# Three small edits in a one-core hybrid encoder step: an earlier weight cast, ten moved sums, other PSUM banks for one product

## The chip, the cores and the metric

The kernel runs on one core of one Trainium2 chip. The metric is device time in microseconds: the median of several runs without a profiler. The core has five engines that run side by side, each through its own queue in order: TensorE (PE in the profile; its weight loads are PEld), VectorE (DVE), ScalarE (ACT), GpSimd (POOL) and SyncE (SP), which here only issues DMA transfers. Matmuls write into PSUM, which has eight banks of 2 KB for each of 128 partitions; all else lives in SBUF or in DRAM.

## The reference

One layer of a streaming encoder, applied to 1024 prompt frames and 32 sample frames that share the weights. Width D = 1024, all in float32:

```python
h = rms_norm(x, g_mix)
q, k, v, ch, cb, cc, ga, gb = split(h @ w_in)           # 1024 x 6656
a = window_attention(q, k, v, sink) @ w_attn_out         # 16 heads, 4 kv heads, ALiBi, sink
conv = causal_conv3(cc * ch)
bo = (cb * conv) @ w_conv_out
x = x + (sigmoid(ga) * a + sigmoid(gb) * bo) @ w_mix_out
hc = rms_norm(x, g_cross)
x = x + softmax(cq(hc) @ mem_k) @ mem_v @ w_co           # 4 heads over 256 memory tokens
hm = rms_norm(x, g_mlp)
x = x + square(relu(hm @ w_up)) @ w_down                 # hidden 4096
y = rms_norm(x, g_final)
```

Besides y it returns the last K and V rows, the last rows of the convolution's input and the memory's K and V.

## The kernel before, in words

**Tiling.** Activations stand with features on the 128 partitions and frames along the free axis, in three chunks of 384, 384 and 288 frames (`CH`). A feature block f is 128 features, so there are eight for each chunk. Every float32 product is made of three matmuls in a shorter float format: weights and activations are each split into a high part (`hi`, `wh`) and a low part (`lo`, `wl`), and hi x hi, hi x lo and lo x hi are added (`gemm`, `product`). A split is one ScalarE cast (L120) and one VectorE subtraction (L121). A weight block of 128 x 1024 is 512 KB; its raw form comes by SP into `wr` (two buffers), its parts go into `wh` and `wl` (three buffers each).

**Order.** Python code writes out the program in full; a planner (the tile framework's scheduler, with a simulated timeline) then sets each engine's order by the program's order and by what is ready in its simulation, and puts in the waits. What it sets is static: on the chip an engine waits at the head of its queue. `plan` is a list of items with the weights that they need; `next_w` issues weights two ahead. `events` is a hand-written table of 48 slots (16 products of three chunks each) beside which the attention units, copies and sums are put.

**Stages.** First the norm, Q, K, V and the memory's K and V; then the 16 products of `hosts`, with attention beside them; then the *input pairs*; then attention's output, convolution's output, mix and cross-attention chunk by chunk; then the up and down projections.

**Input pairs.** Fifteen pairs (`XP`) of output blocks of `w_in` are computed for the two chunks of 384 in a Strassen-Winograd manner: seven products in place of eight. `x_sums` makes from the activations the sums N3, N1, T2 and N4, `x_split` splits them. For a pair, `x_fetch` loads two raw weights (`wr`, and `wr2`), `pair_sums` makes two sums of weights (`s31` and `s24`, one buffer each; VectorE lines 866 and 869, POOL lines 867 and 868), and `x_issue(i, which)` splits weight 1 or 2 (the raw ones), 3 (`s31`) or 4 (`s24`). Weight 2 has buffers of its own; 1, 3 and 4 use the three `wh` and `wl`. `x_p1` and `x_p2` are the first and second half of a product with weight 1, `x_c2(i, half)` is the plain product of the third chunk, in the PSUM tag `pt`. `x_pair` does the rest: weight 4 with T2, weight 3 with N1 and N3, weight 4 with the second chunk's own activations, weight 2 with N4. `x_start` runs ahead: it does weight 1's work for pairs 0 and 1, which `x_pair` then leaves out by `early`. Names such as `x_issue(2, 1)` take the pair and the weight.

**Sums in DRAM.** The down projection needs sums of blocks of `w_down` (`wsum_d`). They are made in DRAM: per block four copies by SP and five DMA transfers by POOL that add what they read to what stands there (L736), 512 KB each, 40 in all. They are kept in program order by `pin`, and each waits for those that it builds on.

**PSUM.** In all stages up to the down projection the eight banks are `acc` (3 buffers of one bank), `pt` (2), `s` (one tile of two banks, scores of attention) and `o` (one bank, attention's values).

**Cross output product.** `do_co(c, half)` computes four feature blocks of the product with `w_co`, two at a time, for chunk c; VectorE adds each to the residual (L1276), and the squares are summed by ScalarE and POOL (`square_acc`, L250 and L252) for the next norm. For the second chunk (c = 1) the two halves run beside the last mix products of the third chunk.

Of the kernel before, what the change touches and what calls it, by code (L numbers as in the profile page):

```python
# [10 lines left out]
F32 = mybir.dt.float32  # L11
# [7 lines left out]
P = 128  # L19
# [19 lines left out]
def hybrid_step(ctx: ExitStack, tc: tile.TileContext, io):  # L39
# [5 lines left out]
    def nm(s):  # L45
        uid[0] += 1
        return f"{s}_{uid[0]}"

    def opened(name, **kw):
        cm = tc.tile_pool(name=name, **kw)  # L50
        return cm, cm.__enter__()

    def closed(cm):
        cm.__exit__(None, None, None)
# [7 lines left out]
    ps_cm, ps = opened("ps", bufs=1, space=PSUM)  # L62
# [28 lines left out]
    def acc_tile(shape):  # L91
        return ps.tile(shape, F32, tag="acc", bufs=n_acc, name=nm("acc"))
# [148 lines left out]
    def square_acc(x, f, c, on_pool=False):  # L241
        n = CH[c][1]
        if f == 0:
            accs[c] = [xacc[0][:, CH[c][0] : CH[c][0] + n]]
        acc = accs[c][0]
        sq = tmp(n) if f else acc
        if on_pool:
            pool_e.tensor_tensor(sq, x, x, op=ALU.mult)
        else:
            act.activation(sq, x, AF.Square)  # L250
        if f:
            pool_e.tensor_tensor(acc, acc, sq, op=ALU.add)  # L252
# [473 lines left out]
    def at(slot, fn):  # L726
        events.setdefault(slot, []).append(fn)
# [14 lines left out]
    adds = [x for s in range(len(sums) + 2) for ph in (2, 1, 0) if 0 <= s - ph < len(sums) for x in sums[s - ph][1][ph]]  # L742
# [12 lines left out]
            at(base + 11, lambda kv=kv: do_KS_rest(kv + 1))  # L755
    for i, x in enumerate(copies):
        at(2 + i, x)
    for i, x in enumerate(adds):
        at(8 + i, x)
    at(38, lambda: x_raw(0))  # L760
    at(40, lambda: x_sums(0))
    at(42, lambda: x_raw(1))
# [39 lines left out]
    def x_raw(k):  # L802
        if k == 0:
            two = [at_tile([P, NT], F32R, t, 2).bitcast(F32) for t in ("KSh", "KSl")]
        elif k == 1:
            two = [C["pool"].tile([P, 1060], F32, tag="u", name=nm("u")), at_tile([P, 4, 256], F32, "bias").rearrange("p h k -> p (h k)")]
        else:
            two = [S["xk"].tile([P, 768], F32, tag="xk", bufs=4, name=nm("xk")) for _ in range(2)]
        xr[k] = b12, b22, b11, b21 = [t[:, a : a + 384] for t in two for a in (0, 384)]
        for t, c, f in ((b12, 1, k), (b22, 1, k + 4), (b11, 0, k), (b21, 0, k + 4)):  # L810
            sp.dma_start(t, io[f"x{c}"][:, f])
# [37 lines left out]
    def pair_issue(key, which):  # L849
        if which == 4 and len(raws[key]) == 2:  # L850
            pair_sums(key)
        src = {1: 0, 2: 1, 3: 2, 4: 3}[which]
        if which == 2:
            hi, lo = (PW["pool"].tile([P, 1024], F32R, tag=t, name=nm(t)) for t in ("wh2", "wl2"))
        else:
            hi, lo = (wp.tile([P, 1024], F32R, tag=t, name=nm(t)) for t in ("wh", "wl"))
        split(hi, lo, raws[key][src])
        wset[key, which] = (hi, lo)
# [22 lines left out]
    def resume():  # L881
        if worder[wpos[0]] is STOP:
            wpos[0] += 1
        issue_w()
# [8 lines left out]
    def x_fetch(i):  # L893
        if i < len(XP):
            pair_fetch(("x", i), *(io["w_in"][in_col(t)] for t in XP[i]))

    def x_issue(i, which):
        if i < len(XP):
            pair_issue(("x", i), which)
        elif which != 2:  # L900
            resume()
# [14 lines left out]
    def x_p1(i):  # L916
        A = acc_tile([P, 384])
        product(A, x_w(i, 1), 0, [x11(k) for k in range(4)], True)
        s1 = xs1[i] = PW["pool"].tile([P, 384], F32, tag="s1", bufs=2, name=nm("s1"))
        act.copy(s1, A)  # L920
        return A

    def x_p2(i, A):
        product(A, x_w(i, 1), 1, [x21(k) for k in range(4)], False)
        x_put(i, 0, 0, A)

    def x_c2(i, half):
        if i >= len(XP) - LATE:
            return
        a = ps.tile([P, CH[2][1]], F32, tag="pt", bufs=2, name=nm("pa"))  # L930
        gemm(a, x_w(i, 1 + half), xg[2])
        x_put(i, half, 2, a)
# [36 lines left out]
    def x_steps(i):  # L969
        if i == 0:  # L970
            todo = {"B11": lambda: x_issue(1, 4), "W4": lambda: x_issue(1, 3), "W2": lambda: [x_issue(1, 2), x_fetch(2), x_issue(2, 1)]}
        elif i == 1:
            todo = {"W4": lambda: x_issue(2, 4), "W3": lambda: x_issue(2, 3), "W2": lambda: x_issue(2, 2)}
        else:
            todo = {f"W{k}": lambda k=k: x_issue(i + 1, k) for k in (1, 4, 3, 2)}
            todo["B11"] = lambda: x_fetch(i + 1)

        def after(what):
            todo.get(what, lambda: None)()
            if what == "B11" and XP[i][0][0] == "a" and "cv_cm" in S:  # L980
                closed(S.pop("r2_cm"))
                closed(S.pop("cv_cm"))
                G["pool"] = ctx.enter_context(tc.tile_pool(name="gb", bufs=5, reuse_waits="tile", side="right"))

        return after

    def x_start():
        x_issue(0, 4)
        A = x_p1(0)
        x_issue(0, 3)  # L990
        x_c2(0, 0)
        x_p2(0, A)
        x_issue(1, 1)
        x_c2(0, 1)
        A = x_p1(1)
        x_p2(1, A)
        x_c2(1, 0)
# [16 lines left out]
    item(do_in(("b", 1), ex, (1, 0, 2)), ("w_in", in_col(("b", 1))))  # L1014
    worder.append(STOP)
    item(x_start)
    def open_r2():
        closed(S.pop("xk_cm"))
# [82 lines left out]
    def gain_split(x, g, c):  # L1101
        hi, lo = yslot(c), yslot(c)
        scaled_split(hi, lo, x, g)
        return hi, lo
# [63 lines left out]
    qc, co = {}, [[None, None] for _ in CH]  # L1168
# [91 lines left out]
    def do_co(c, half):  # L1260
        def fn(w):
            n = CH[c][1]
            wh, wl = w
            fs = range(4 * half, 4 * half + 4)
            for f in fs:
                if f % 2 == 0:
                    two = [acc_tile([P, n]) for _ in range(2)]
                    for k, g in ((k, g) for k in range(2) for g in range(2)):
                        s = slice((((f + g) % 4) * 2 + k) * P, (((f + g) % 4) * 2 + k) * P + P)
                        hi, lo = co[c][k]  # L1270
                        pe.matmul(two[g], wh[:, s], hi, start=(k == 0), stop=False)
                        pe.matmul(two[g], wh[:, s], lo, start=False, stop=False)
                        pe.matmul(two[g], wl[:, s], hi, start=False, stop=(k == 1))
                a = two[f % 2]
                x = x1[c][f]
                dve.tensor_add(x, a, x)  # L1276
                if half == 0 and c == 2:
                    xm[c][f] = gain_split(x, G_MLP + f, c)
                square_acc(x, f, c)
            if half == 1 and c == 2:  # L1280
                for f in fs:
                    xm[c][f] = gain_split(x1[c][f], G_MLP + f, c)

        return fn
# [668 lines left out]
```

## Time and profile before

| | |
|---|---|
| median of 3 runs | 1770.37 us (1770.33 to 1771.17) |
| the profiled execution's own time | 1778.77 us |
| its span, first to last instruction | 1776.7 us |
| mean granted TensorE clock | 0.995 |
| TensorE, VectorE, ScalarE, POOL busy | 98%, 67%, 48%, 30% |
| matmuls | 11012 |
| HBM over the span | 199 GB/s |

The profile is one execution with the hardware profiler on. Busy shares are averages over stages that differ; the granted clock is the share of TensorE's full clock that its throttle let through. A matmul row of 384 columns lasts 0.33 us, but the next one starts after 0.17, since matmuls overlap. In the prediction times on the timeline count from the span's start, and an idle time in brackets is that of the engine just before the row, with what ended it.

### The profile page before, as it was taken

How to read it: one execution, taken by the hardware profiler on the slowest of the kernel's cores; microseconds unless marked ns; L12 is line 12 of the kernel's file. 1: busy time of each engine (PE TensorE's matmuls, PEld its weight loads, DVE VectorE, ACT ScalarE, POOL GpSimd, SP SyncE). 2: the span in 40 equal slices, each digit the busy share in tenths (PEclk: the TensorE clock that was granted, in tenths of full speed). 3: DMA queues.
4: the chain of work that ended last, by engine and by line, in shares of the span. 5: the costliest groups of instructions: out<-in, count | busy, mean ns of one | idle time of the engine just before them, and what ended most of it. 6: DMA issues, size and time to landing. Idle time of an engine off the chain costs nothing.

```text
span 1776.7 us, 29946 instructions
## 1 busy us (share of the span) xinstructions
PE 1739.0 (98%) x11012; PEld 1716.6 (97%) x11012; DVE 1198.0 (67%) x2130; ACT 846.6 (48%) x1625; POOL 540.0 (30%) x550
## 2 busy tenths in 40 slices
PE   9999999999999999999999999999999999999998
PEld 8999999999999999999999889999999998999997
DVE  6768878666786767457675867766666676445675
ACT  8667767852232245244455755642222343333553
POOL 2245564542342210003323242375555300100111
PEclk9999999999999999999999999999999999999999
DMA  5428997771221416478766767744434596444673
GB/s 182 157 94 236 253 233 197 170 201 62 73 72 49 135 49 212 153 260 285 265 203 213 234 211 240 265 158 143 143 124 134 161 304 211 163 152 146 225 242 134
DMA packets 151107, 317.21 MB, mean 179 GB/s; under 512 B 18320, under 2 KB 105136, under 8 KB 150320
## 3 DMA queue, kind: packets, MB, share of 16 engines
q1 hardware_dynamic: 145056, 294.27, 49.3%
q0 software_dynamic: 5760, 20.97, 6.7%
q8 instruction: 87, 1.43, 0.3%
q14 instruction: 60, 0.49, 0.1%
q10 hardware_dynamic: 144, 0.05, 0.0%
HBM read 254.20 MB, written 98.78 MB: 199 GB/s over the span
## 4 chain that ended last, share of the span: by engine, by line
PE 82%; DMA 5%; DVE 4%; ACT 4%; issue 2%; POOL 2%; SPq 0%; POOLq 0%; DVEq 0%; ACTq 0%
PE acc L176 9%; PE acc L175 9%; PE acc L177 9%; PE acc L877 7%; PE acc L878 7%; PE acc L879 7%; PE acc L1686 6%; PE acc L1685 6%; PE acc L1684 6%; PE pa L176 3%; PE pa L175 3%; PE pa L177 3%; DVE wl L121 1%; PE pt L587 1%; DMA ct<-m_d 1%
## 5 line engine op out<-in xcount | busy, mean ns | idle before, releaser
L120 ACT CAST wh<-wr 128x1024 fp32r<-128x1024 f32 (+1 forms) x224 | 234.3, 1046 | 320.1 <-PE acc L1685 85.0
L121 DVE TENSOR_TENSOR wl<-wr,wh 128x1024 fp32r<-128x1024 f32 (+1 forms) x224 | 304.1, 1358 | 102.3 <-ACT wh L120 101.2
L175 PE MATMUL acc<-Y,wh 128*128 128x384 f32 (+1 forms) x624 | 201.6, 324 | 0.8 <-DVE ct L1327 0.6
L176 PE MATMUL acc<-Y,wh 128*128 128x384 f32 (+1 forms) x624 | 201.8, 323 | 0.0
L177 PE MATMUL acc<-Y,wl 128*128 128x384 f32 (+1 forms) x624 | 201.6, 323 | 0.0
L252 POOL TENSOR_TENSOR xacc<-xacc,ct 128x384 f32<-128x384 f32 (+1 forms) x62 | 77.6, 1252 | 328.3 <-ACT ct L250 325.9
L175 PE MATMUL acc<-X,wh 128*128 128x384 f32 (+1 forms) x528 | 172.8, 327 | 0.0
L176 PE MATMUL acc<-X,wh 128*128 128x384 f32 (+1 forms) x528 | 171.6, 325 | 0.4 <-DVE X L256 0.4
L177 PE MATMUL acc<-X,wl 128*128 128x384 f32 (+1 forms) x528 | 171.3, 324 | 0.0
L175 PEld LDWEIGHTS acc<-Y,wh 128*128 128x128 f32 x624 | 117.1, 188 | 1.4 <-DVE ct L1327 0.8
L177 PEld LDWEIGHTS acc<-Y,wl 128*128 128x128 f32 x624 | 117.2, 188 | 0.2 <-DVE wl L121 0.2
L176 PEld LDWEIGHTS acc<-Y,wh 128*128 128x128 f32 x624 | 117.2, 188 | 0.0
L577 POOL TENSOR_SCALAR S<-S,rec 128x256 f32<-128x256 f32 (+1 forms) x96 | 90.3, 956 | 80.7 <-DVE rec L574 80.7
L1684 PE MATMUL acc<-Y,wh 128*128 128x384 f32 (+1 forms) x352 | 113.0, 321 | 0.0
L1686 PE MATMUL acc<-Y,wl 128*128 128x384 f32 (+1 forms) x352 | 112.9, 321 | 0.0
L1685 PE MATMUL acc<-Y,wh 128*128 128x384 f32 (+1 forms) x352 | 112.9, 321 | 0.0
L120 ACT CAST wh<-s 128x1024 fp32r<-128x1024 f32 x54 | 56.7, 1051 | 106.9 <-PE acc L878 72.3
L176 PEld LDWEIGHTS acc<-X,wh 128*128 128x128 f32 x528 | 100.1, 190 | 2.3 <-DVE X L256 1.5
L175 PEld LDWEIGHTS acc<-X,wh 128*128 128x128 f32 x528 | 100.1, 190 | 1.5 <-ACT X L255 0.3
L177 PEld LDWEIGHTS acc<-X,wl 128*128 128x128 f32 x528 | 100.0, 189 | 0.6 <-DVE wl L121 0.2
L1118 POOL TENSOR_TENSOR sgl<-sgl,ct 128x384 f32<-128x384 f32 (+1 forms) x21 | 22.2, 1056 | 227.1 <-DVE sgl L1115 167.6
L121 DVE TENSOR_TENSOR Y<-ct,Y 128x384 fp32r<-128x384 f32 (+1 forms) x128 | 66.7, 554 | 35.0 <-ACT Y L120 34.8
(401 smaller groups left out, 5287.7 us busy)
## 6 DMA issues: line engine op xcount, KB each, us to landing
wr<-in_w_in SPq DMA_DIRECT2D x55, 512.0 KB, 3.4
wr<-in_w_up SPq DMA_DIRECT2D x48, 512.0 KB, 4.0
wsum_d<-in_w_down SPq DMA_DIRECT2D x32, 512.0 KB, 6.2
wr<-in_w_down SPq DMA_DIRECT2D x32, 512.0 KB, 3.6
wr<-wsum_d SPq DMA_DIRECT2D x32, 512.0 KB, 3.4
wl<-wl_d SPq DMA_DIRECT2D x28, 512.0 KB, 5.0
wsum_d<-in_w_down POOLq DMA_DIRECT2D x24, 512.0 KB, 7.7
wr<-in_w_conv_out SPq DMA_DIRECT2D x24, 512.0 KB, 5.1
```

Source lines behind the costliest of these rows:

```text
L120: act.copy(hi, src)
L121: dve.tensor_sub(lo, src, hi.bitcast(F32))
L175: pe.matmul(out, wh[:, a], hi, start=(k == 0), stop=False)
L176: pe.matmul(out, wh[:, a], lo, start=False, stop=False)
L177: pe.matmul(out, wl[:, a], hi, start=False, stop=(k == len(acts) - 1))
L577: pool_e.tensor_scalar_mul(stl[:, h, :nk], stl[:, h, :nk], rec[:, h : h + 1])
L877: pe.matmul(acc, wh[:, a], hi, start=(start and k == 0), stop=False, skip_group_check=True)
L878: pe.matmul(acc, wh[:, a], lo, start=False, stop=False, skip_group_check=True)
L879: pe.matmul(acc, wl[:, a], hi, start=False, stop=(k == 3), skip_group_check=True)
L1684: pe.matmul(a, wh[:, s], hi, start=(start and k == 0), stop=False, skip_group_check=True)
L1685: pe.matmul(a, wh[:, s], lo, start=False, stop=False, skip_group_check=True)
L1686: pe.matmul(a, wl[:, s], hi, start=False, stop=(stop and k == len(acts) - 1), skip_group_check=True)
```

## The change

1. `x_start` casts pair 1's first weight before anything else, and pair 0's third weight (`x_issue(0, 3)`) after `x_p2(0)`; before, pair 0's fourth and third came first and pair 1's first after `x_p2(0)`.
2. Of the 40 adding transfers only the first 30 stand in the table of slots (8 to 37; before 8 to 47). The last ten are issued one each at the end of input pairs 1 to 10, after that pair's last issue.
3. In `do_co` for c = 1, each half's four products take two banks of one `s` tile, the `o` bank and one `acc` buffer; before, four `acc` buffers in turn. The other chunks keep `acc`.

```diff
-    for i, x in enumerate(adds):
-        at(8 + i, x)
+    for i in range(30):
+        at(8 + i, adds.pop(0))
...
         def after(what):
             todo.get(what, lambda: None)()
+            if i and what == "W2" and adds:
+                adds.pop(0)()
...
     def x_start():
+        x_issue(1, 1)
         x_issue(0, 4)
         A = x_p1(0)
-        x_issue(0, 3)
         x_c2(0, 0)
         x_p2(0, A)
-        x_issue(1, 1)
+        x_issue(0, 3)
         x_c2(0, 1)
         A = x_p1(1)
         x_p2(1, A)
...
-                    two = [acc_tile([P, n]) for _ in range(2)]
+                    if c != 1:
+                        two = [acc_tile([P, n]) for _ in range(2)]
+                    elif f % 4 == 0:
+                        both = ps.tile([P, 4, 256], F32, tag="s", name=nm("co")).rearrange("p b t -> p (b t)")
+                        two = [both[:, :n], both[:, 512 : 512 + n]]
+                    else:
+                        two = [ps.tile([P, n], F32, tag="o", name=nm("co")), acc_tile([P, n])]
```

## The prediction

> **What bounds the kernel.** I read the page first, then TensorE's own waits, then the timeline at each long wait, then busy time by windows. Columns of a timeline row: start us, length us, engine, line, operation, tiles, shape, count, and in brackets the idle time before it and what ended it. A row of waits has total us, times, longest us.
>
> ```profile
> PE 1739.0 (98%) x11012; PEld 1716.6 (97%) x11012; DVE 1198.0 (67%) x2130; ACT 846.6 (48%) x1625; POOL 540.0 (30%) x550
> ...
> PE acc L877 <- ACT wh L120: 4.8, 2, 3.5
> PE acc L1271 <- DVE Gb L1276: 4.0, 3, 2.1
> ...
> PE acc L1684 <- DVE Ga L1674: 2.0, 1, 2.0
> ...
> PE acc L1271 <- DVE Ga L1276: 1.2, 2, 1.0
> ...
> PE o L599 <- DVE AO L606: 1.1, 1, 1.1
> ...
> PE acc L879 <- DVE wl L121: 0.7, 1, 0.7
> ```
>
> TensorE is busy 1739.0 of a span of 1776.7 us, so what can be won is idle TensorE time, 37.7 us in all, and matmuls that run below full clock. The longest single wait, 3.5 us, is for a weight cast in the input pairs (L877); the next, 2.1 us, is in the cross output product (L1271), the second chunk's as the timeline shows. The change touches both places. The three edits are costed by themselves.
>
> **Edit 1: the second pair's cast moves to the front.** The wait and its neighbourhood:
>
> ```profile
> 386.18 0.33 PE L879 MATMUL acc<-X,wl 128*128 128x384 f32 x1
> ...
> 390.52 0.69 PE L877 MATMUL acc<-X,wh 128*128 128x384 f32 x1 [3.48 <-ACT wh L120]
> ...
> 387.60 0.44 ACT L677 ACTIVATE ct<-ct 128x288 f32<-128x288 f32 x1 [3.27 <-DVE ct L676]
> 388.59 0.93 ACT L834 CAST tk<-xk 128x384 fp32r<-128x384 f32 x2 [0.55 <-DVE xk L822]
> 389.43 1.04 ACT L120 CAST wh<-wr 128x1024 fp32r<-128x1024 f32 x1
> ...
> 393.73 0.90 DVE L836 TENSOR_TENSOR tk<-xk,tk 128x384 fp32r<-128x384 f32 x1
> ...
> 394.92 1.66 DVE L121 TENSOR_TENSOR wl<-wr,wh 128x1024 fp32r<-128x1024 f32 x1
> ...
> 339.11 0.38 SPq L845 DMA_DIRECT2D wr<-in_w_in  x1
> ```
>
> There are three `wh` buffers. At x_start they hold the weights of `b`,3 and `b`,1, which come free early, and pair 0's first weight, which `x_p2(0)` reads last (its last row: 386.18). Before, `x_issue(0,4)` and `x_issue(0,3)` take the two early ones, and the cast for pair 1 has to take the third, after 386.5. There it stands in ScalarE's order behind L677 and two L834, each waiting for VectorE, and is done at 390.47. Its raw weight was asked for at 339.11, fifty us earlier, so data is not the limit. With the new order pair 1 gets an early buffer and TensorE can go on at 390.52 - 3.48 = 387.04: 3.48 us (0 to 3.48; I take all, because nothing else of `x_p1(1)` is missing).
>
> The clock, by windows (busy us of each engine with its count, then granted clock, DMA share, GB/s):
>
> ```profile
> 390.52:393.83 3.31, 3.31 (x11) 3.31 (x12) 3.31 (x4) 0.87 (x2) 3.23 (x3) 0.50 0.17 52
> 393.83:400.00 6.17, 6.17 (x40) 6.17 (x39) 3.22 (x4) 2.62 (x6) 1.67 (x2) 1.00 0.40 141
> 1482.65:1489.50 6.85, 6.29 (x19) 5.78 (x20) 5.56 (x11) 1.01 (x3) 0.00 (x0) 0.50 0.72 233
> ...
> 1482.65 0.62 PE L1684 MATMUL acc<-H,wh 128*128 128x384 f32 x1 [2.02 <-DVE Ga L1674]
> ```
>
> Right behind the idle time the granted clock is 0.50 for 3.31 us. At full clock that work takes half: 3.31 x 0.5 = 1.66 us more to win (0 to 1.66; I take 1.66). [...]
>
> What is late next: the cast of `x_issue(0,3)`, moved past `x_c2(0,0)` and `x_p2(0)`, now waits for the third buffer and inherits about the old place: cast near 389.4, low part on VectorE until 394.92 + 1.66 = 396.58 at the latest. TensorE first has 12 matmuls of `x_p1(1)`, 12 of `x_p2(1)`, 24 of `x_c2(1,0)` and 12 with T2; at 6.17/40 = 0.154 us each these 60 end at 387.04 + 9.3 = 396.3. T2 and N1 operands are done at 393.73 + 0.90 = 394.6. So it is covered within 0.3 us, if the scheduler keeps that order. VectorE has one low part fewer in this stretch, since pair 1's goes before it. The edit moves no DMA issue, but pair 1's sums write the buffer that `x_issue(0,3)` reads; they start later, as does what SP fetches once they are done.
>
> ```profile
> 388.95 0.68 DVE L866 TENSOR_TENSOR s<-wr 128x512 f32<-128x512 f32 x1
> ...
> 430.34 1.49 POOL L868 TENSOR_TENSOR s<-wr,s 128x512 f32<-128x512 f32 x1
> ...
> 404.03 1.05 ACT L120 CAST wh<-s 128x1024 fp32r<-128x1024 f32 x1 [4.71 <-PE acc L878]
> ...
> 406.99 0.45 PE L879 MATMUL acc<-tk,wl 128*128 128x384 f32 x1 [0.74 <-DVE wl L121]
> ```
>
> The wait of 0.74 us at 406.99 is for pair 1's fourth weight, cast at 404.03 only when `x_p2(1)` gave its buffer back. `x_p2(1)` now runs earlier, so the buffer no longer ends this wait; the sums may. If pair 0's third low part ends at 396.58, one VectorE sum (0.68, as at 388.95), POOL's two (1.49 each, as the one at 430.34), the cast (1.05) and its low part (1.66) put this weight at 402.9. TensorE, done with T2 at 396.3, reaches pair 1's T2 at 396.3 + 24 x 0.154 = 400.0 if it keeps the old order, and at 403.7 if the two other products of pair 0 go first. So from 0.74 us won to 2.9 us lost; I take 0, since the planner sees the wait coming and has the two products to put there.
>
> **Edit 2: ten sums move.** Each moved sum is one DMA of 512 KB that adds in memory, issued by POOL.
>
> ```profile
> 339.91 0.85 POOL L736 DMA_DIRECT2D wsum_d<-wsum_d  x1
> ...
> 353.65 0.81 POOL L736 DMA_DIRECT2D wsum_d<-in_w_down  x1 [3.01 <-DMA wsum_d<-wsum_d]
> ...
> 342.74 1.03 SPq L811 DMA_DIRECT2D bias<-in_x  x2
> ...
> 349.34 0.62 DVE L821 SCALAR_TENSOR_TENSOR u<-bias,prm,u 128x384 f32<-128x384 f32 x1 [4.17 <-DMA bias<-in_x]
> ...
> 351.18 0.84 DVE L606 TENSOR_TENSOR AO<-o,tO 64x256 f32<-64x256 f32 x2
> ...
> 352.17 0.47 PE L599 MATMUL o<-PTh,VS 128*128 128x512 f32 x1 [1.09 <-DVE AO L606]
> ...
> DMA to landing us min/median/max: 2.6/4.5/6.7
> 340.00:350.00 10.00, 10.00 (x68) 9.74 (x67) 5.01 (x16) 9.35 (x19) 5.71 (x9) 1.00 0.88 205
> 440.00:460.00 20.00, 20.00 (x126) 20.00 (x125) 17.11 (x25) 7.04 (x10) 10.87 (x13) 1.00 0.18 61
> ```
>
> At 342.74 SP asks for rows of x that land at 349.3, the slowest kind of this line's (the landing row is L811's). VectorE stands 4.17 us, L606 is queued behind it, and TensorE waits 1.09 us for its bank. The sum at 339.91 moves in the same stretch, with DMA share 0.88; without it I expect the line's median, 4.5 us, thus 2 us earlier, and the 1.09 us goes (0 to 1.09, taken whole). In the pairs the ten cost POOL 10 x 0.85 = 8.5 us. POOL has 9 us free in 440 to 460, DMA share is 0.18, TensorE is busy without a gap there. I take 0; bounds 0 and 8.5 if each came straight onto TensorE. A speed-up there is excluded, since there is no idle time to remove. [...]
>
> **Edit 3: idle banks for the second chunk's product.**
>
> ```profile
> 1030.07 0.44 PE L1271 MATMUL acc<-Y,wh 128*128 128x384 f32 x1 [1.03 <-DVE Ga L1276]
> ...
> 1035.09 0.45 PE L1273 MATMUL acc<-Y,wl 128*128 128x384 f32 x1 [0.19 <-DMA wl<-wl_d]
> ...
> 1040.22 0.44 PE L1271 MATMUL acc<-Y,wh 128*128 128x384 f32 x1 [2.07 <-DVE Gb L1276]
> ...
> 1027.74 0.42 SPq L148 DMA_DIRECT2D wl<-wl_d  x1
> ...
> 1038.65 1.05 DVE L256 SCALAR_TENSOR_TENSOR Y<-Gb,prm,Y 128x288 fp32r<-128x288 f32 x1
> 1039.62 1.47 DVE L1276 TENSOR_TENSOR Gb<-acc,Gb 128x384 f32<-128x384 f32 x3
> ...
> 1040.92 5.16 POOL L252 TENSOR_TENSOR xacc<-xacc,ct 128x384 f32<-128x384 f32 x4 [1.55 <-ACT ct L250]
> ```
>
> In each half the fourth product waits for VectorE to empty a bank of the three (1.03 and 2.07 us). With two products in `s`, one in `o` and one in `acc`, none waits for another of its half. Second half: 2.07 us gone. First half: 1.03 us gone, but the next half stands at 1035.09 for the low weights landing there, asked for at 1027.74 in SP's order; TensorE would reach that point 1.03 us earlier and wait longer. So 0 of it, bounds 0 to 1.03. What is late next: the sums of squares (L252) end at 1046.08, and TensorE comes 2.07 us earlier to the statistics that read them.
>
> **Sum.** 3.48 + 1.66 + 0 + 1.09 + 0 + 2.07 = 8.30 us. The profiled execution took 1778.77 us, 2.07 beyond its span and 8.40 above the median of the runs, so it gives 1770.5, and carried over to the median: 1770.37 - 8.30 = 1762.1 us, 0.47% less.
>
> **Rivals.**
> - The moved cast only trades places. Cast (0,3) becomes the late one, if the static order puts the N1 product ahead of pair 1's second half as the old order did. Edit 1 is lost whole: 1770.37 - 1.09 - 2.07 = 1767.2. For it: VectorE is the laggard here. Against: the cover of 9.3 us worked out above.
> - Part of the sum is missing in the timed runs. Either edit 3 is eaten by the same low weights (1762.1 + 2.07 = 1764.2), or the half clock at 390.52 was this execution's alone. The two stretches last 3.31 and 6.85 us, about one and two steps of 3.4; if the steps lie otherwise in a timed run, the idle time falls across two of them, and there may be no 1.66 to win: 1763.7. [...]
> - The other half-clock stretch goes too. Shifted by 8 us, the 2.02 us gap at 1482.65 may not trip the clock: another 6.85 x 0.5 = 3.4 us, 1758.7. The reverse, a smaller gap that newly trips it, costs the same kind of sum.
> - New order, new waits: the planner reorders downstream and 5 us or more of the gain is eaten in small waits: 1767 to 1770.
> - Slower: a moved sum waits at the head of POOL's in-order queue for the one before it to land, as the 3.01 us at 353.65 shows, with the pair's own sums (L867, L868) behind it, and these feed the casts of weights.
>
> ```profile
> 438.28 1.05 ACT L120 CAST wh<-s 128x1024 fp32r<-128x1024 f32 x1 [0.89 <-PE pa L176]
> ```
>
> POOL's second sum ends at 431.83, so the cover is 438.28 - 431.83 = 6.4 us. A wait of 3.01 plus 0.81 stays inside it; it would have to come beside others to leave, say, 3 us uncovered in each of ten pairs: 1762.1 + 30 = 1792. It decides from (8.30 + 3.54)/10 = 1.18 us uncovered a pair. Against: the sums stand a pair, some 20 us, apart.
>
> **How the numbers follow.** 0.2% is 3.54 us, about what a measurement of this kernel tells from no change: faster is below 1766.8. Forecast as summed 0.40; part missing 0.21; second half-clock stretch gone too 0.14; traded places 0.12; new waits 0.07; slower 0.06. Faster 0.75, same 0.19, slower 0.06. The range 1757.0 to 1769.0 holds the first three and the traded place, and most of the new waits; for the likeliest alone it is 1760.3 (all of edit 3 and the 0.74) to 1765.0 (2.9 us lost to pair 1's fourth weight).
>
> **What would show it.** Right: no TensorE wait over 1 us from 380 to 410 and clock 1.00 there; pair 1's first cast before 380; the L821 wait well under 4.17; no L1271 wait on L1276 in the second chunk's product, and a longer one on `wl`; ten L736 rows among the pairs with TensorE 20.00 of 20. Wrong: a wait on L120 or L121 for pair 0's third weight, POOL waiting for a landing in the pairs, or new half-clock stretches.

## The result, and the profile after

| | median | ratio to the kernel before, 95% interval |
|---|---|---|
| before | 1770.7 us | |
| changed | 1757.93 us (1757.3 to 1759.29) | 0.9929 [0.9912, 0.9946] |

The change makes the kernel 12.6 us faster (9.6 to 15.6). Forecast were 8.3 us, 1762.1, in a range from 1757.0 to 1769.0. The direction holds, and the time is near the lower end of the range: the change won about half as much again as the sum says. Which term was too small is the question of the runs below. The profiled execution of the changed kernel took 1757.3 us, with a span of 1755.5.

From its page, the busy time of the engines:

```profile
PE 1731.5 (99%) x11012; PEld 1712.2 (98%) x11012; DVE 1198.0 (68%) x2130; ACT 846.4 (48%) x1625; POOL 545.1 (31%) x550
```

From TensorE's waits (total us, times, longest us):

```profile
PE acc L1279 <- DVE Gb L1284: 1.9, 2, 1.3
...
PE acc L877 <- ACT wh L120: 1.3, 1, 1.3
...
PE pq L206 <- POOL xacc L252: 0.7, 1, 0.7
...
PE acc L877 <- DVE lt L950: 0.6, 1, 0.6
```

L1279 and L1284 are the old L1271 and L1276. The 1.9 us left there are the first and the third chunk's. The wait of L877 for ScalarE's cast, 3.5 us before, is gone from the input pairs: the 1.3 us in this row lie at 1173 us, in the up projection. Of work that became late next there are two small waits, both in these rows: the sums of squares (L206, 0.70 us), which the prediction named, and a plain operand of the pairs (L950, 0.65 us), which it did not.

The timeline of ScalarE around `x_start`, and busy time and clock by windows:

```profile
362.83 1.05 ACT L120 CAST wh<-wr 128x1024 fp32r<-128x1024 f32 x1 [1.74 <-PE acc L176]
...
377.86 1.04 ACT L120 CAST wh<-s 128x1024 fp32r<-128x1024 f32 x1
...
386.42 1.05 ACT L120 CAST wh<-s 128x1024 fp32r<-128x1024 f32 x1
...
394.16 1.05 ACT L120 CAST wh<-s 128x1024 fp32r<-128x1024 f32 x1 [1.80 <-POOL s L868]
```

```profile
384.00:396.00 12.00, 12.00 (x79) 12.00 (x78) 9.25 (x15) 6.71 (x13) 7.83 (x6) 1.00 0.18 57
396.00:408.00 12.00, 11.35 (x66) 11.03 (x65) 8.03 (x13) 3.57 (x4) 3.10 (x2) 1.00 0.12 46
```

Pair 1's first weight is cast at 362.83, 26.6 us earlier than before. Pair 0's third (386.42) and pair 1's fourth (394.16) now come last, and TensorE waits for neither: it is busy 12.00 of 12.00 us from 384 to 396, at clock 1.00.

### The profile page after: what moved, and what is told of

Read it like the earlier page. It is cut to its first block, busy times and chain, and to the rows that moved or that the text cites. A ratio compares the mean times of both kernels' runs of the same rounds, so it can differ in the third digit from the quotient of the medians.

```text
span 1755.5 us, 29939 instructions
## 1 busy us (share of the span) xinstructions
PE 1731.5 (99%) x11012; PEld 1712.2 (98%) x11012; DVE 1198.0 (68%) x2130; ACT 846.4 (48%) x1625; POOL 545.1 (31%) x550
## 4 chain that ended last, share of the span: by engine, by line
PE 83%; DMA 6%; DVE 4%; ACT 3%; issue 2%; POOL 1%; SPq 0%; POOLq 0%; DVEq 0%; ACTq 0%
PE acc L176 9%; PE acc L175 9%; PE acc L177 9%; PE acc L877 7%; PE acc L879 7%; PE acc L878 7%; PE acc L1693 6%; PE acc L1692 6%; PE acc L1694 6%; PE pa L176 3%; PE pa L177 3%; PE pa L175 3%; DVE wl L121 2%; PE pt L587 2%; DMA ct<-bc_d 1%
## 5 line engine op out<-in xcount | busy, mean ns | idle before, releaser
L120 ACT CAST wh<-s 128x1024 fp32r<-128x1024 f32 x54 | 56.7, 1051 | 105.4 <-PE acc L878 70.4
L120 ACT CAST Y<-ct 128x384 fp32r<-128x384 f32 (+1 forms) x128 | 59.0, 486 | 62.8 <-DMA ct<-bc_d 21.1
```

The lines of the kernel that those rows point to most:

```text
L120: act.copy(hi, src)
```

## The experiments

Every kernel was timed in turns with the kernel before on the same chip; a gain in us is 1 minus the ratio, times 1771.

**The kernel before, once more, and each edit alone.**

> The kernel before, unchanged, for a second profile of it. Theory A (the 8.4 us by which the first profiled execution lay above the median are waits and half-clock stretches that not every execution has): the new span lies at 1768 to 1771, the 3.48 us wait in x_start and its half clock are there again (they are set by the program's order), and what is missing is the stretch around 1470 to 1490 (2.0 us gap, 6.85 us at half clock). Theory B (the profiler itself costs 8 us): span near 1776.7 again, with both half-clock stretches. Ratio to the kernel before 1.000 in both.

Measured: ratio 1.0004 [0.9990, 1.0017]. Its profile tells how much the places of the sum vary between executions of one program:

```profile
392.70 0.69 PE L877 MATMUL acc<-X,wh 128*128 128x384 f32 x1 [4.31 <-ACT wh L120]
```

The wait for the cast is 4.31 us here and 3.48 in the prediction's row; the clock is 0.50 for 6.83 us behind it, not 3.41; and the stretch at 1482 is missing. The span is 1770.2 us, so the profiler by itself does not cost the 8 us by which the first profiled execution lay above the median.

> Edit 1 alone: pair 1's first weight cast first, pair 0's third after x_p2(0). My prediction: 3.48 + 1.66 = 5.1 us less, ratio 0.9971, no granted clock below 1.00 between 380 and 410. Rival 'trades places': within 1 us of before, with a wait of 3 us for pair 0's third weight. Rival 'half clock is this execution's alone': 3.5 us less.

```diff
 def x_start():
+    x_issue(1, 1)
     x_issue(0, 4)
     A = x_p1(0)
-    x_issue(0, 3)
     x_c2(0, 0)
     x_p2(0, A)
-    x_issue(1, 1)
+    x_issue(0, 3)
```

Measured: 0.9962 [0.9947, 0.9976], 6.7 us faster (4.3 to 9.4). No half clock there, and of the wait only small ones are left, the longest 0.76 us.

> Edit 2 alone: the last ten adding transfers at the end of pairs 1 to 10. My prediction: 1.1 us less (the L599 wait at 352), ratio 0.9994; cost in the pairs 0. Rival: the sums in the pairs cost TensorE up to 8.5 us, ratio up to 1.005. Rival from the result, that the whole was 4 us better than the sum of my terms because of this edit: 4 to 5 us less, with L821 waiting under 2 us and less waiting elsewhere in 330 to 400.

```diff
-    for i, x in enumerate(adds):
-        at(8 + i, x)
+    for i in range(30):
+        at(8 + i, adds.pop(0))
...
+            if i and what == "W2" and adds:
+                adds.pop(0)()
```

Measured: 0.9988 [0.9976, 1.0000], 2.1 us (0 to 4.3). The wait at L599 is gone. Unforeseen, this edit also shortened the wait that edit 1 is for, though the order of the casts is the old one:

```profile
387.63 0.45 PE L877 MATMUL acc<-X,wh 128*128 128x384 f32 x1 [2.28 <-ACT wh L120]
```

In the same profile the wait at edit 3's place (2.02 us) is followed by half clock from 1034.78 to 1038.20, and there is half clock again from 1478.51 to 1481.93.

> Edit 3 alone: s, o and one acc bank for the second chunk's cross output product. My prediction: 2.1 us less, ratio 0.9988, first half's 1.03 us lost again to the low weights' landing. Rival: both halves count and the low weights land earlier as well, 3.9 us less (the step seen between 1000 and 1050 when the two profiles are laid on each other), ratio 0.9978. Rival: the sums of squares (L252) take the place of the banks and under 1 us is left.

```diff
-                    two = [acc_tile([P, n]) for _ in range(2)]
+                    if c != 1:
+                        two = [acc_tile([P, n]) for _ in range(2)]
+                    elif f % 4 == 0:
+                        both = ps.tile([P, 4, 256], F32, tag="s", ...)
+                        two = [both[:, :n], both[:, 512 : 512 + n]]
+                    else:
+                        two = [ps.tile([P, n], F32, tag="o", ...), acc_tile([P, n])]
```

Measured: 0.9970 [0.9960, 0.9981], 5.3 us (3.4 to 7.1), well over the 2.07. The three alone add up to 14.1 us, the whole change won 12.6.

**Each edit undone in the changed kernel.** In the builds with edit 1 alone and with edit 3 alone, the planner also put the start of the down projection in another order, the changed kernel's; with edit 2 alone it kept the old one. Undoing one edit leaves the changed kernel's order there, so this bias is out of the next three.

> The changed kernel with edit 1 undone; its down projection starts in the changed kernel's order, so that what is lost against the changed kernel is edit 1's alone. The prediction's term: 5.14 us (3.48 idle and 1.66 at half clock), so some 1763 us. The theory after the runs so far (idle time at this wait of 2.3 to 4.5 us, then 0, 3.4 or 6.8 us at half clock): 6.5 us on average, 1764.4. The rival that edit 1's -6.7 us as measured alone was in part the other order at the down projection: 5 us or less, 1763.

```diff
-        x_issue(1, 1)
         x_issue(0, 4)
         A = x_p1(0)
+        x_issue(0, 3)
         x_c2(0, 0)
         x_p2(0, A)
-        x_issue(0, 3)
+        x_issue(1, 1)
```

Measured: 1764.5 us, 0.9964 [0.9951, 0.9978]. Against the changed kernel's 0.9929 the edit is worth 0.0035, 6.2 us (2.4 to 10.0, from both intervals). The wait, again with edit 2 in place, is short and no half clock follows in the profiled execution. That one took 1761.7 us, 2.8 under the median; whether the slower ones had half clock here no profile shows.

```profile
388.76 0.44 PE L877 MATMUL acc<-X,wh 128*128 128x384 f32 x1 [2.40 <-ACT wh L120]
```

> The changed kernel with edit 3 undone, the down projection in the changed kernel's order. The prediction's term: 2.07 us lost, 1760.0. The theory after the runs so far (both halves' waits come back, 1.0 and 0.6 to 2.1, less the 0.5 to 0.9 us that TensorE otherwise waits for the sums of squares): 1.0 to 2.5 us, 1759 to 1760.5, where edit 3 alone had measured 5.3 us, of which the rest was the order at the down projection. If edit 3 by itself is worth 4 us or more: 1762 or above.

```diff
-                    if c != 1:
-                        two = [acc_tile([P, n]) for _ in range(2)]
-                    elif f % 4 == 0:
...
+                    two = [acc_tile([P, n]) for _ in range(2)]
```

Measured: 1762.94 us, 0.9955 [0.9940, 0.9970], 4.6 us lost (0.6 to 8.6). The waits of both halves are back:

```profile
1019.81 0.44 PE L1273 MATMUL acc<-Y,wh 128*128 128x384 f32 x1 [1.02 <-DVE Ga L1278]
1028.04 0.45 PE L1273 MATMUL acc<-Y,wh 128*128 128x384 f32 x1 [0.61 <-DVE Gb L1278]
```

> The changed kernel with edit 2 undone, the down projection in the changed kernel's order. The prediction's term: 1.1 us lost, 1759, with TensorE's wait on AO (L606) before 360 us back. Rival: this wait comes and goes between executions (0.0 to 1.3 us), and the ten transfers cost nothing in the input pairs: 0 to 1 us. If the ten cost something there, undoing them wins that back: under 1757.9.

```diff
-    for i in range(30):
-        at(8 + i, adds.pop(0))
+    for i, x in enumerate(adds):
+        at(8 + i, x)
...
-            if i and what == "W2" and adds:
-                adds.pop(0)()
```

Measured: 1762.01 us, 0.9951 [0.9939, 0.9963], 3.9 us lost (0.2 to 7.6), over both expectations, though its interval holds both. The wait at L599 did not come back (none over 0.15 us there), so the loss lies elsewhere, and the trace shows where. First the windows, of this kernel and of the changed one (the last two columns are DMA share and GB/s; a transfer counts whole where it starts, so that a share can pass 1):

```profile
350.00:360.00 10.00, 10.00 (x61) 9.69 (x60) 7.69 (x16) 7.26 (x12) 3.75 (x6) 1.00 0.95 176
360.00:370.00 10.00, 10.00 (x66) 9.78 (x65) 3.66 (x7) 6.08 (x14) 4.41 (x4) 1.00 1.06 242
```

```profile
350.00:360.00 10.00, 10.00 (x61) 9.48 (x61) 5.57 (x11) 6.99 (x13) 0.00 (x0) 1.00 0.16 52
360.00:370.00 10.00, 10.00 (x67) 10.00 (x66) 6.95 (x13) 6.51 (x15) 4.99 (x4) 1.00 0.20 63
```

With the ten sums in the slots the DMA engines are full from 350 to 370; without them they are four fifths idle. Next, how long the stores of attention's output (L607, `ao_d`) take to land in that stretch, sums in the slots, then sums moved:

```profile
DMA to landing us min/median/max: 1.6/8.7/11.9
```

```profile
DMA to landing us min/median/max: 1.6/1.8/1.8
```

And what waits for them, on VectorE and in SP's queue, sums in the slots (two fences) and moved (two more):

```profile
370.10 0.45 DVE L606 TENSOR_TENSOR AO<-o,tO 64x64 f32<-64x64 f32 x2 [3.53 <-DMA ao_d<-AO]
...
376.90 0.69 DVE L866 TENSOR_TENSOR s<-wr 128x512 f32<-128x512 f32 x1 [3.17 <-DMA wr<-in_w_in]
```

```profile
370.58 0.37 SPq L607 DMA_DIRECT2D ao_d<-AO  x1
...
373.17 0.33 SPq L846 DMA_DIRECT2D wr<-in_w_in  x1
```

```profile
365.44 0.45 DVE L606 TENSOR_TENSOR AO<-o,tO 64x64 f32<-64x64 f32 x2 [0.30 <-ACT tO L604]
...
373.07 0.69 DVE L866 TENSOR_TENSOR s<-wr 128x512 f32<-128x512 f32 x1 [0.78 <-DMA wr<-in_w_in]
```

```profile
365.92 0.37 SPq L607 DMA_DIRECT2D ao_d<-AO  x1
...
369.34 0.33 SPq L846 DMA_DIRECT2D wr<-in_w_in  x1
```

The chain reads: sums fill the DMA engines; a store of `AO` takes up to 11.9 us; VectorE stands 3.53 us because the buffer is not free; the next store goes out at 370.58 and not at 365.92; behind it in SP's order stands pair 0's second raw weight, asked for 3.8 us later; the sums of weights start 3.8 us later. The two executions are 1.4 us apart before this place, so about 2.4 us of it is the sums' doing. All of `x_start` that hangs on these operands moves with it. At its end stands ScalarE's copy of a product out of its bank (L920), for which TensorE waits, here 1.04 us and once before 0.25; sums in the slots, then moved, where TensorE does not wait for this copy:

```profile
393.33 0.46 ACT L920 COPY s<-acc 128x384 f32<-128x384 f32 x1
...
393.85 0.44 PE L877 MATMUL acc<-X,wh 128*128 128x384 f32 x1 [1.04 <-ACT s L920]
```

```profile
389.51 0.46 ACT L920 COPY s<-acc 128x384 f32<-128x384 f32 x1
```

With edit 1 alone the same two waits are there (0.34 and 0.76 us). So the work that edit 1 reorders was late in part because of the transfers that edit 2 moves.

**The order at the start of the down projection.** Here the profiles of before and after differ most beyond the places of the edits. On VectorE before:

```profile
1478.89 1.75 DVE L1520 TENSOR_TENSOR fold<-fold,fold 128x384 f32<-128x384 f32 x3 [5.60 <-DMA fold<-b_d]
1480.56 0.55 DVE L1674 TENSOR_TENSOR Ga<-acc,Ga 128x384 f32<-128x384 f32 x1
```

VectorE stands 5.60 us at the head of its queue for operands from DRAM, and the adds that empty the output banks (L1674) stand behind; TensorE waits 2.02 us for them, and half clock follows. In the changed kernel's order the adds come ahead of the last of these subtractions. To price the order alone, a few matmuls on constants were put ahead of the last two up pairs: they change the planner's timeline, and with some counts its order at this place.

> All three edits, plus eight 128x128 matmuls on constants ahead of the last two up pairs, whose only other effect is that the planner puts the start of the down projection in the order of the kernel before: the last subtraction of the folded operands ahead of the adds that empty the output banks. The eight cost about 0.1 us each on TensorE, 0.8 us. Theory O (the order is worth time): the wait on L1674's add, 1.3 to 2.0 us, is back, with the one for the low weights behind it, 0.6 to 0.9, perhaps with a half clock stretch (1.7 to 3.4 more): 1.9 to 6 us slower than the changed kernel besides the 0.8, so some 1761 to 1765, and a gap of over 1 us near 1465 in the profile. Theory N (no order effect, the gain there was a matter of executions): the changed kernel's time plus 0.8, 1758.7, and no such gap.

> The control of the run with the old order: all three edits and four of the same matmuls in the same place, with which the planner keeps the changed kernel's order at the down projection. Both theories: the changed kernel's time plus 0.4 us, 1758.3, and no gap over 0.5 us from 1430 to 1480 in the profile. If it comes out like the run with the old order, the order is not the cause.

```diff
...
+    item(lambda: dummies(8))      # old order;  kept order: dummies(4)
     item(lambda: up_last(len(UP) - 2))
```

Measured: old order 1760.34 us, 0.9925 [0.9912, 0.9939]; kept order 1758.94 us, 0.9921 [0.9908, 0.9933]. Of the 1.4 us between them 0.4 are the four matmuls, so the order is worth about 1 us here, within both intervals. With the old order VectorE does stand ahead of the adds again, but only for 2.97 us, and TensorE's wait for the adds did not return:

```profile
1464.51 0.56 DVE L1528 TENSOR_TENSOR fold<-fold,fold 128x384 f32<-128x384 f32 x1 [2.97 <-DMA fold<-b_d]
...
1466.54 0.55 DVE L1688 TENSOR_TENSOR Ga<-acc,Ga 128x384 f32<-128x384 f32 x1
```

With the kept order the adds go first, and the subtractions' 4.17 us behind them cost nothing:

```profile
1460.02 0.55 DVE L1688 TENSOR_TENSOR Ga<-acc,Ga 128x384 f32<-128x384 f32 x1
1464.73 0.56 DVE L1528 TENSOR_TENSOR fold<-fold,fold 128x384 f32<-128x384 f32 x1 [4.17 <-DMA fold<-b_d]
```

So the order matters when the loads are slow, and they were slow in the prediction's profile (5.60 us), in its repeat (4.88) and with edit 2 alone (4.53). The control missed its expectation in one point: a wait of 0.83 us for low weights stayed at 1466.

> None of the three edits: the kernel before with twenty of the same matmuls ahead of the last two up pairs (about 2 us on TensorE), which makes the planner take the changed kernel's order at the start of the down projection. Theory O: the waits of 1.3 to 2.0 and 0.6 to 0.9 us at the adds and any half clock behind them go; time is 2 us up and 2 to 5 down: 1767.5 to 1771, with no gap over 1 us near 1480 in the profile. Theory N: 1770.7 + 2.0 = 1772.7 and the gap stays.

```diff
 # the kernel before
...
+    item(lambda: dummies(20))
     item(lambda: up_last(len(UP) - 2))
```

Measured: 1771.26 us, 0.9996 [0.9987, 1.0005]. The twenty take 2.1 us on TensorE (1371.5 to 1373.6) and the time does not rise (0.7 us less, from 0.9 more to 2.3 less), so the order gives that back and perhaps a little more; no wait for the adds in its profile, 0.73 us for low weights. Together: 1 to 3 us for the order, at the edge of what can be measured.

**Half of edit 3.**

> Edit 3 for the first half of the second chunk's product alone; the second half keeps its acc buffers. In this build the down projection comes in the new order. The step of the prediction (the first half's 1.03 us is lost again to low weights that land late, 0 us): the wait on wl in the second half's first product grows from 0.2 to about 1.2 us, and only the order's 2 to 3 us are won: 1768. The rival (the late landing was that execution's alone, since in other executions the same load lands 4.3 us after its issue and TensorE does not wait for it): no wait on wl over 0.3 us, 1.0 us more is won, or less if the second half's wait of 0.6 to 2.1 us for an emptied bank grows by the same 1 us: 1767 to 1768. The profile tells them apart, the time hardly does.

```diff
-                    two = [acc_tile([P, n]) for _ in range(2)]
+                    if not (c == 1 and half == 0):
+                        two = [acc_tile([P, n]) for _ in range(2)]
+                    elif f % 4 == 0:
...
```

Measured: 1767.19 us, 0.9973 [0.9962, 0.9985]. TensorE waits for no low weights in the second half. They landed 4.3 us after their request, 4.2 in the repeat of the kernel before, and 7.3 in the prediction's profile. The wait grew where the rival put it, at an `acc` bank behind the second half:

```profile
1035.45 0.41 PE L175 MATMUL acc<-Y,wh 128*128 128x384 f32 x1 [1.61 <-DVE Gb L1282]
```

**The clock by itself.**

> The kernel before with 32 matmuls of 128x128 on constants ahead of pair 1's first product, in the place of the idle time (about 0.1 us each, 3.4 us together, into the idle bank pair of the scores). They take none of the wait for the cast away. Its down projection starts in the changed kernel's order, worth 1 to 2 us. Theory C (half clock follows from the idle time): granted clock 1.00 from 385 to 400 us, the wait left under 1.2 us, and 1.7 or 3.4 us less time there than in the kernel before: 1767 to 1769. Theory T (half clock comes by the time of the run, whatever TensorE does): a stretch of 3.4 or 6.8 us at 0.50 here as before, and 1769.5 to 1770.5.

```diff
         x_c2(0, 1)
+        fill = ps.tile([P, 4, 256], F32, tag="s", ...).rearrange("p b t -> p (b t)")
+        for _ in range(32):
+            pe.matmul(fill[:, :P], ones_r, ones_r, start=True, stop=True)
         A = x_p1(1)
```

Measured: 1770.13 us, 0.9997 [0.9987, 1.0008]: no gain, against the 2 to 4 us of theory C. The wait for the cast shrank to 0.32 us and no half clock followed it, as theory C has it. But the low part of the same weight was late, and behind this new wait came a half clock of its own:

```profile
391.33 0.44 PE L877 MATMUL acc<-X,wh 128*128 128x384 f32 x1 [0.32 <-ACT wh L120]
...
397.45 0.69 PE L879 MATMUL acc<-X,wl 128*128 128x384 f32 x1 [1.80 <-DVE wl L121]
```

So in these two kernels half clock followed idle time, 3.48 us of it before and 1.80 us here. What its removal is worth this kernel does not show, because TensorE's order changed too: 16 matmuls with `tk` stand between the first rows of this weight's high part and its low part, where the kernel before has 24. At 0.17 us each the missing eight make about 1.4 of the 1.80 us. The other 0.4 stays with all 24 ahead: with edit 2 alone, and with edit 1 undone, where TensorE runs there at full clock, the low part is 0.42 and 0.41 us late, and in the kernel before not at all. So of time at half clock a little would be lost again behind it.

## Why the prediction was right, and where its sizes were off

| | forecast | timed alone | timed undone | at its place in the traces |
|---|---|---|---|---|
| edit 1 | 5.14 | 6.7 (4.3 to 9.4) | 6.2 (2.4 to 10.0) | 4.0 |
| edit 2 | 1.09 | 2.1 (0 to 4.3) | 3.9 (0.2 to 7.6) | 2.1, and 0 to 1.8 at L599 |
| edit 3 | 2.07 | 5.3 (3.4 to 7.1) | 4.6 (0.6 to 8.6) | 2.2 |
| sum | 8.30 | 14.1 | 14.7 | 8.3, and 0 to 1.8 |

The timed columns are wide; edits 1 and 3 alone hold the other order of the down projection too, so that their sum counts it twice, and the three of the next column share the uncertainty of the changed kernel's own time. The last column is narrower. TensorE issues the same matmuls in every kernel, in another order only inside the edited stretches, so the time between two matmuls by number can be compared across profiles.

- From the 2500th to the 2960th matmul (381 to 456 us in the changed kernel): 80.5 to 82.2 us in five kernels with neither edit 1 nor edit 2, 77.3 and 77.5 with edit 1 and the sums in the slots, 79.2 and 79.3 with edit 2 and the old casts, 75.3 and 75.4 in four kernels with both. So edit 1 is worth about 4.0 here and edit 2 about 2.1, each with or without the other.
- From the 6400th to the 6660th (the second chunk's product, 1010 to 1051 us): 43.3 to 43.7 us in five kernels with the old banks, 45.5 in the prediction's execution and 46.3 with edit 2 alone, where half clock follows; 41.2 to 41.8 in six with the new banks.
- From the 8500th to the 9600th (into the down projection, 1345 to 1519 us): 176.7, 177.5 and 180.4 us in three kernels with the old order, 173.4 to 175.1 in eight with the new one.

The forecast of 8.30 and the 8.3 of the last column agree by accident: edit 1 was taken 1 us too high, edit 2 as much too low. What the change won beyond them is the wait at L599, where an execution has it, and the order.

**Edit 1.** The mechanism is shown: both the wait and the half clock go with the new order, alone and in the whole. The cover for pair 0's third weight held, with its cast at 386.42 instead of the 389.4 taken from the old row, and the rival of traded places fell. In the changed kernel the 0.74 us wait for pair 1's fourth weight went, and 0.65 us for a plain operand came in the same place, so the 0 for this step was right by accident. But "what is late next" missed ScalarE's copies (L920): with the sums in the slots TensorE waits for them, and the edit alone gave 3.2 us of the 5.14 in the execution the term was read from (80.5 to 77.3), and up to 4.9 in others. Only with edit 2 as well does it come to 5.1 (75.4). In the five profiles with neither edit 1 nor edit 2 the wait was 3.5 to 4.5 us, with 3.41 or 6.83 us at half clock behind it, so the rival "half clock of this execution alone" fell.

**Edit 2.** This is the step that failed in its cause. The prediction saw the rows of x that land late at 349 and the 1.09 us at L599. That wait varies from none to 1.8 us in kernels with all sums in the slots: none with edit 1 alone, edit 3 alone, the new order alone and edit 2 undone, 0.4 with half of edit 3, 1.3 in the repeat of the kernel before, 1.8 in the filled one. What the edit takes away in every profile is the full DMA engines from 350 to 370 (share 0.84 to 1.07 in the eight with the sums in the slots, 0.15 to 0.22 in the six with them moved), and with it the late stores of `AO` that held up VectorE and SP. The prediction read only the window from 340 to 350. The cost of the ten in the pairs was 0, as taken: all ten are issued between 408 and 591, and on POOL they take 0.81 to 0.91 us each. So it is from 440 to 460 too, where two of them are issued (0.83 and 0.81) with VectorE busy 19.12 of 20.00 us, and TensorE stays busy:

```profile
440.00:460.00 20.00, 20.00 (x128) 20.00 (x127) 19.12 (x28) 6.33 (x11) 13.73 (x18) 1.00 0.49 117
```

**Edit 3.** The term of 2.07 came out near 2.2, by two errors that cancel. The second half's 2.07 us is the upper end: the wait is 2.02 with edit 2 alone and 0.86 with edit 1 alone, but 0.61 to 0.65 in four other profiles with the old banks. The first half's 1.0 us, taken as 0, is won in the changed kernel, which waits nowhere in this product; the low weights' late landing was one execution's alone. 0.70 us is lost again at L206. The 5.3 timed for the edit alone fits these 2.2 us and the 1 to 3 of the down projection's order; the 4.6 of the edit undone does not hold the order, and for what it has beyond 2.2 no cause is shown, but its interval reaches down to 0.6.

**What was left out.** The planner's new order at the down projection, some 400 us behind the last edit, 1 to 3 us. The prediction had reordering downstream only as a loss. The other half-clock rival (1758.7, the stretch at 1482 goes too) came true in the trace and near in the time, but the stretch comes and goes: of three profiles with the old order and no added matmuls one has 6.83 us of it, one (edit 2 alone) 3.41, and the repeat none. So it is a gain in some executions only.

## What to carry to other kernels

Read the DMA share for the whole stretch from a moved transfer to the next long wait, not just around the wait that it visibly ends: here, with edit 2 undone, the share from 350 to 370 was 0.95 to 1.06, a store of `AO` took up to 11.9 us to land in place of 1.8, and VectorE stood 3.53 us for one at 370. A wait of one profile has a range, 3.48 and 4.31 us for the same cast in two executions of the kernel before; profile the unchanged kernel twice before pricing an edit at its exact length. A change in one place can reorder a planned program elsewhere: compare the static orders of the two builds and price the difference on its own. Where timed intervals are too wide, compare the time between the same two matmuls in many profiles.

## What the hardware showed that was not expected

**In these traces half clock comes in steps of 3.413 us, and it followed windows with 1.52 us or more of idle time.** The shortest half-clock stretch of the kernel before lasts 3.413 us, the next one 6.827. They start at 390.42 and 1482.69, 1092.27 us or 320.0 steps of 3.413 apart, and the one at the kernel's end starts at 1769.41, 84.0 steps later. With edit 2 alone the starts at 1034.78 and 1478.51 are 443.73 us apart, 130.0 steps. So windows of this length can be laid on a trace, with an edge where a half-clock stretch starts, and TensorE's busy time read in each. Before (the first window in each pair, then the one behind it, with its clock):

```profile
387.01:390.42 3.41, 0.03 (x1) 0.00 (x0) 3.41 (x8) 2.27 (x5) 0.65 (x1) 1.00 0.88 139
390.42:393.83 3.41, 3.31 (x11) 3.31 (x12) 3.41 (x4) 0.97 (x3) 3.33 (x3) 0.50 0.21 60
1479.28:1482.69 3.41, 1.39 (x12) 1.18 (x10) 3.34 (x8) 1.04 (x1) 0.00 (x0) 1.00 0.56 203
1482.69:1486.10 3.41, 2.85 (x8) 2.34 (x9) 3.41 (x8) 0.00 (x0) 0.00 (x0) 0.50 0.41 125
```

The repeat of the kernel before, where idle time fell into two windows and two at half clock followed; last two rows, the place where half clock followed in the other execution, here 1.49 us idle with full clock behind it:

```profile
387.02:390.43 3.41, 1.36 (x9) 1.13 (x8) 3.41 (x5) 0.44 (x1) 2.02 (x2) 1.00 0.30 30
390.43:393.84 3.41, 1.14 (x4) 1.15 (x5) 3.41 (x5) 2.29 (x4) 1.82 (x2) 0.50 0.85 180
393.84:397.26 3.42, 3.42 (x13) 3.42 (x12) 3.42 (x6) 1.10 (x3) 3.42 (x3) 0.50 0.00 0
1475.86:1479.28 3.42, 1.93 (x13) 1.40 (x11) 3.38 (x8) 1.04 (x1) 0.00 (x0) 1.00 0.52 190
1479.28:1482.69 3.41, 2.69 (x15) 2.69 (x16) 3.41 (x8) 0.00 (x0) 0.00 (x0) 1.00 0.64 212
```

Edit 1 alone, early in the kernel, the window with the least idle time (1.52 us) that was followed by half clock:

```profile
71.58:74.99 3.41, 1.89 (x14) 1.49 (x14) 2.46 (x6) 1.52 (x5) 0.00 (x0) 1.00 0.75 196
74.99:78.40 3.41, 3.41 (x17) 3.41 (x18) 0.16 (x1) 0.81 (x1) 0.00 (x0) 0.50 0.90 322
```

Edit 1 undone, where a gap of 2.40 us is cut in two by a window's edge, and nothing follows:

```profile
384.27:387.68 3.41, 2.09 (x14) 1.86 (x12) 3.41 (x5) 1.29 (x4) 2.12 (x2) 1.00 0.14 48
387.68:391.10 3.42, 2.34 (x14) 2.32 (x14) 3.42 (x4) 1.96 (x4) 3.01 (x2) 1.00 0.00 0
```

At half clock, less idle time was followed by more of it. Before, the window from 1482.69, at half clock with 2.85 us busy and 0.56 idle, was followed by another at half clock; in the kernel with the new order alone, 2.90 us busy and 0.51 idle were followed by full clock:

```profile
389.53:392.94 3.41, 0.00 (x0) 0.00 (x0) 3.41 (x7) 1.86 (x4) 0.49 (x2) 1.00 0.72 115
392.94:396.35 3.41, 2.90 (x10) 2.90 (x11) 3.41 (x4) 1.38 (x3) 3.33 (x3) 0.50 0.33 84
```

Between start-up and the kernel's end, windows at full clock with 1.52 us or more without a matmul were followed by half clock, those with 1.50 or less were not (1.50 from 72.98 to 76.39 in the kernel before), with one exception: in the filled kernel a window with 1.77 us idle (349.69 to 353.10) was followed by full clock. Why is open. At the kernel's end half clock also followed windows with less, 0.74 us idle with edit 3 alone, and that is open too. So the length of a gap alone did not settle it here: 2.02 us inside one window were followed by half clock at 1482.69, 2.40 us cut in two at 387.68 were not.

**Stores landed late beside the sums.** With the DMA engines at 0.95 to 1.06 of their time (edit 2 undone, 350 to 370), stores of `AO` that land in 1.8 us otherwise took up to 11.9. So it is in all 14 profiles: from 350 to 372 the median store takes 7.7 to 9.5 us in the eight with the sums in the slots and 1.8 in the six others.
